# The opening of a two-layer attention encoder: zeros ahead of the first matmul, another queue for the norm weights, smaller first weight chunk, a fixed order

## The chip, the core and the metric

The kernel runs on one core of one Trainium2 chip. The core has five engines with a program each: TensorE (PE: matmuls, transposes), VectorE (DVE), ScalarE (ACT), GpSimd (POOL), and SyncE (SP), which issues most of the DMAs. An engine works through its own instructions in a fixed order and waits for others by semaphores. The metric is the device time of one execution in microseconds; lower is better.

## The reference

Two layers over 512 frames of width 1024. Each normalises its input by the root of the mean of squares, mixes the frames, adds the result, and then does the same with a wide squared-ReLU MLP. Layer 0 mixes by sparse attention: an indexer scores all keys for each query, the best 128 are kept, and 16 heads attend to those. Layer 1 is latent attention. A last norm follows. What the change touches is the start of layer 0:

```python
def rms_norm(x, g):
    xf = x.astype(jnp.float32)
    y = xf * lax.rsqrt(jnp.mean(xf * xf, axis=-1, keepdims=True) + EPS)
    return (y * g.astype(jnp.float32)).astype(x.dtype)

def dsa_mixer(h, w_in, w_out, cos_a, sin_a, cos_i, sin_i):
    proj = h @ w_in                                   # 512 x 1024 @ 1024 x 2120
    q, k, v, qi, ki, wi = jnp.split(proj, cuts, axis=-1)
    ...
    logits = jnp.einsum('bthd,bsd->bths', qib, ki, preferred_element_type=f32)
    score = jnp.einsum('bths,bth->bts', jax.nn.relu(logits), wib)
    _, sel = lax.top_k(score, top_k)
```

## The kernel before

The 512 frames lie in four tiles of 128 rows, worked in the order 1, 2, 3, 0. All weights and activations are split in a high and a low part of a shorter float type, and each product is three matmuls (`mm3`): high by high (L227), high by the weight's low part (L228), low by the weight's high part (L229). In the names of the profile, `w_hi` and `w_lo` are the parts of a weight chunk, `hT_hi` and `hT_lo` those of the activations with the features on the partitions.

`Weights` brings the weights in, chunk after chunk, in a list that `rows` fills. `fetch` starts the load of the next chunk into one of three raw buffers. `convert` makes the parts: ScalarE casts the high part (L143), and GpSimd ("ap") or VectorE ("av") subtracts it to get the low part (L150); there are five buffers for parts. `take` hands out the next chunk and converts others ahead of need, `held` fewer than the buffers would allow. The first three chunks hold the rows 0 to 2, 3 to 5 and 6 to 7 (of eight rows of 128) of 292 columns of `a_w_in`, the next three the same rows of 292 more.

The opening, in the code's order: loads of tile 1, of the norm weights (`g_row`, one row of 1024) and of the other tiles and chunks on SyncE's queue (L301 to L309); `g_ps` (L316): two matmuls with a row of ones spread the norm weights over 128 partitions; the constants `ident`, `smask`, `inv`. Then, for each tile, `gains` (L477, VectorE) multiplies by the norm weights into `h`; `turn` transposes `h` on TensorE by eight 128 x 128 transposes into `tps` (L454), ScalarE copies `hT_hi` from there (L458) and VectorE subtracts `hT_lo` (L459); `factor` lets ScalarE sum the squares (L483, `junk`), VectorE take the mean (L484, `lead`), and GpSimd the power -1/2 (L485). `idx_rows` projects tiles 1, 2 and 3 on the first 292 columns into the banks `ip`; `out_of` (L715) moves a finished `ip` to `inat`, scaled by the factor. `rope_tables` makes the rotary tables from the positions (L337 to L374: `posf`, `pos`, `ang`, `turns`, `sincos`). After that `idx_tile` projects the second 292 columns (64 of them for tile 0), then `proj_tiles` the remaining columns (`pp`); index scores (`lp`) come between, and the selection and the heads follow.

A scheduler in the framework orders each engine's instructions by data, priority and estimated times; the code's order is only where it starts from. The rest of the program is two MLPs and the second mixer, which the change doesn't touch.

## Time and profile before

| what | us |
|---|---|
| median of 3 runs | 1151.42 (1150.63 to 1152.6) |
| the profiled execution | 1150.95 |
| its span, from the first to the last instruction seen | 1149.2 |
| TensorE busy | 1117.5 |
| VectorE busy | 754.8 |
| GpSimd busy | 670.0 |
| ScalarE busy | 619.7 |

A row of a timeline names the start, the duration, the engine, the line, the operation and what it writes and reads; at its end stand the engine's idle time before it and what ended it. Matmuls are pipelined, so the distance of two starts (the pitch) tells more than the duration of one. The granted clock (PEclk) is a share of 2.4 GHz.

### The profile page before, as it was taken

What the parts mean: (1) busy time and instruction counts of PE and PEld (TensorE: products, weight loads), DVE (VectorE), ACT (ScalarE), POOL (GpSimd) and SP (SyncE); (2) the same over time, 40 slices, a digit from 0 to 9 for tenths busy, and PEclk for the clock granted to TensorE, in tenths of its full rate; (3) what the DMA queues carried; (4) which work ended last, traced back from release to release, by engine and by line L of the source; (5) the groups of instructions that cost most, each with busy time, mean ns of one, the idle gap of its engine ahead of it and who ended that gap; (6) DMA issues with size and microseconds to landing.
All of it is one profiled execution on the core that took longest, in us unless ns stands there. A gap on an engine that the chain in (4) does not pass through costs nothing.

```text
span 1149.2 us, 16018 instructions
## 1 busy us (share of the span) xinstructions
PE 1117.5 (97%) x5725; PEld 949.2 (83%) x5725; DVE 754.8 (66%) x1399; ACT 619.7 (54%) x1143; POOL 670.0 (58%) x508
## 2 busy tenths in 40 slices
PE   8999899989999999999999999899999999999997
PEld 7788788869888888888889898787988888888886
DVE  6699798673566466466566788676556466556664
ACT  6574896534544554454445776563564454464452
POOL 5498533543657857856702643554557756865772
PEclk9999999989999999999999999999999999999999
DMA  6413100242224314413322200111424313412402
GB/s 200 123 55 110 38 1 1 76 150 87 75 72 147 106 58 130 133 58 103 86 62 79 76 23 34 56 56 56 167 63 138 128 49 117 147 61 87 147 10 83
DMA packets 65465, 99.04 MB, mean 86 GB/s; under 512 B 3173, under 2 KB 41833, under 8 KB 65386
## 3 DMA queue, kind: packets, MB, share of 16 engines
q1 hardware_dynamic: 65386, 98.03, 26.9%
q8 instruction: 45, 0.74, 0.3%
q14 instruction: 34, 0.28, 0.1%
HBM read 95.92 MB, written 2.10 MB: 85 GB/s over the span
## 4 chain that ended last, share of the span: by engine, by line
PE 90%; DVE 3%; ACT 3%; issue 2%; POOL 1%; DMA 1%; SPq 0%; DVEq 0%; POOLq 0%; ACTq 0%
PE dn L1226 23%; PE up L227 10%; PE up L229 10%; PE up L228 10%; PE s_ps L560 3%; PE o_ps L622 3%; PE pt_ps L579 2%; PE wo_ps L227 2%; PE wo_ps L228 2%; PE wo_ps L229 2%; PE pp L227 2%; PE pp L229 2%; PE pp L228 2%; PE tps L454 1%; PE dn L228 1%
## 5 line engine op out<-in xcount | busy, mean ns | idle before, releaser
L148 POOL TENSOR_TENSOR w_lo<-quad,w_hi 128x512 fp32r<-128x512 f32 x196 | 274.7, 1433 | 163.1 <-ACT w_hi L143 155.7
L150 POOL TENSOR_TENSOR w_lo<-w_raw,w_hi 128x1024 fp32r<-128x1024 f32 (+4 forms) x117 | 264.4, 2278 | 86.7 <-ACT w_hi L143 71.6
L1229 DVE TENSOR_TENSOR x<-dn,x 128x512 f32<-128x512 f32 x196 | 134.9, 690 | 139.5 <-PE dn L1226 139.4
L228 PE MATMUL up<-hT_lo,w_hi 128*128 128x512 f32 (+1 forms) x576 | 210.8, 367 | 0.0
L227 PE MATMUL up<-hT_hi,w_hi 128*128 128x512 f32 (+1 forms) x576 | 210.3, 368 | 0.0
L229 PE MATMUL up<-hT_hi,w_lo 128*128 128x512 f32 (+1 forms) x576 | 208.8, 367 | 0.0
L143 ACT CAST w_hi<-w_raw 128x1024 fp32r<-128x1024 f32 (+6 forms) x112 | 111.7, 1006 | 141.1 <-PE dn L1226 62.2
L143 ACT CAST w_hi<-quad 128x1024 fp32r<-128x1024 f32 x98 | 101.2, 1050 | 100.0 <-DVE quad L86 71.7
L1226 PE MATMUL dn<-w_hi,lh 128*128 128x512 f32 x392 | 152.5, 389 | 0.0
L1226 PE MATMUL dn<-w_lo,lh 128*128 128x512 f32 x392 | 152.5, 389 | 0.0
L1226 PE MATMUL dn<-w_hi,ll 128*128 128x512 f32 x392 | 152.5, 389 | 0.0
L1191 DVE TENSOR_TENSOR ll<-u,lh 128x512 fp32r<-128x512 f32 x106 | 99.2, 966 | 40.7 <-ACT lh L1190 40.7
L229 PEld LDWEIGHTS up<-hT_hi,w_lo 128*128 128x128 f32 x576 | 109.1, 190 | 17.6
L227 PEld LDWEIGHTS up<-hT_hi,w_hi 128*128 128x128 f32 x576 | 109.0, 190 | 17.6 <-ACT hT_hi L458 0.2
L228 PEld LDWEIGHTS up<-hT_lo,w_hi 128*128 128x128 f32 x576 | 109.1, 190 | 17.4
L86 DVE TENSOR_TENSOR quad<-quad 128x1024 f32<-128x1024 f32 x56 | 68.4, 1221 | 65.3 <-POOL w_lo L148 65.3
L1190 ACT CAST lh<-u 128x512 fp32r<-128x512 f32 x106 | 62.9, 620 | 75.0 <-DVE u L1203 66.6
L1226 PEld LDWEIGHTS dn<-w_hi,ll 128*128 128x128 f32 x392 | 73.6, 188 | 15.3
L1226 PEld LDWEIGHTS dn<-w_hi,lh 128*128 128x128 f32 x392 | 73.6, 188 | 15.3
L1226 PEld LDWEIGHTS dn<-w_lo,lh 128*128 128x128 f32 x392 | 73.6, 188 | 15.3
L573 ACT ACTIVATE p<-p,m 128x128 f32<-128x128 f32 (+3 forms) x128 | 72.0, 564 | 16.3 <-DVE m L568 15.5
L592 ACT CAST pt_hi<-pt_ps 128x128 fp32r<-128x128 f32 (+3 forms) x128 | 53.0, 423 | 27.8 <-PE pt_ps L579 25.3
(237 smaller groups left out, 2249.8 us busy)
## 6 DMA issues: line engine op xcount, KB each, us to landing
w_raw<-in_mlp_w_up_dram SPq DMA_DIRECT2D x64, 512.0 KB, 3.7
quad<-in_mlp_w_down_dram SPq DMA_DIRECT2D x56, 512.0 KB, 3.6
w_raw<-in_a_w_in_dram SPq DMA_DIRECT2D x12, 512.0 KB, 3.6
w_raw<-in_a_w_out_dram SPq DMA_DIRECT2D x8, 512.0 KB, 3.2
w_raw<-in_mlp_w_down_dram SPq DMA_DIRECT2D x8, 512.0 KB, 4.5
w_raw<-in_b_w_out_dram SPq DMA_DIRECT2D x8, 512.0 KB, 3.7
x<-in_x_dram SPq DMA_DIRECT2D x4, 512.0 KB, 7.5
w_raw<-in_b_w_kv_up_dram SPq DMA_DIRECT2D x4, 512.0 KB, 3.9
```

Of the source, the lines that this page charges most:

```text
L86: self.nc.vector.tensor_sub(q[o], q[l], q[r])
L143: nc.scalar.copy(h, v)
L148: nc.gpsimd.tensor_sub(l[:, cs], v[:, cs], h[:, cs].bitcast(F32))
L150: (nc.gpsimd if engs[1] == "p" else nc.vector).tensor_sub(l, v, h.bitcast(F32))
L227: nc.tensor.matmul(ps, lh, rh, start=first, stop=False)
L228: nc.tensor.matmul(ps, lh, rl, start=False, stop=False)
L229: nc.tensor.matmul(ps, ll, rh, start=False, stop=last)
L573: nc.scalar.activation(U["p"][:, :N], U["p"][:, :N], AF.Exp, bias=U["m"], scale=-1.0, accum_out=pair["sums"][:, c:c + 1])
L1190: nc.scalar.copy(lh, v)
L1191: nc.vector.tensor_sub(ll, v, lh.bitcast(F32))
L1226: nc.tensor.matmul(pp[t], l[:, k, ts], r[:, k, :], start=first and k == 0 and m == 0, stop=k == 1 and m == 2, skip_group_check=True)
L1229: last = nc.vector.tensor_add(x[:, cs], pp[t], x[:, cs])
```

## The change

Seven things are changed, all ahead of the second set of index columns:

1. `smask` is zeroed by VectorE as the first thing, and seven matmuls of 128 x 128 zeros (`rest`) stand on TensorE ahead of `g_ps`.
2. `g_row` and the positions are loaded on ScalarE's queue; `g_row` is that engine's first instruction, ahead of its table load.
3. Tile 1 is loaded in two halves.
4. The first 292 columns come in four chunks, of 1, 2, 3 and 2 rows, in place of three of 3, 3 and 2. The third is subtracted by VectorE ("av"), the others by GpSimd. Two chunks are fetched right behind tile 1.
5. The opening's order on TensorE, ScalarE and VectorE is that of the code. `take(1, 4)` converts the chunk that is taken and none beyond it; `ahead` is new and converts a given number beyond.
6. The sums of squares (`squares`) are apart from mean and power (`factor`) and stand later.
7. The rotary tables are issued behind the last `hT_lo`.

```diff
+    def ahead(self, n):
+        while len(self.done) < min(self.taken + n, len(self.items)):
+            self.convert()
...
+    smask = const.tile([P, 512], F32, name="smask")
+    nc.vector.memset(smask[:, 0:P], 0.0)
+    nc.vector.memset(smask[:, P:512], 0.0)
+    with tc.high_priority(400):
+        rest = bank("rest", 7)
+        for _ in range(7):
+            nc.tensor.matmul(rest[:, 0:P], smask[:, 0:P], smask[:, 0:P], start=True, stop=True)
...
-    W.rows(a_w_in[0][0:3 * P], 1536, 1828, 3, "av")
-    W.rows(a_w_in[0][3 * P:6 * P], 1536, 1828, 3, "ap")
-    W.rows(a_w_in[0][6 * P:8 * P], 1536, 1828, 2, "ap")
+    W.rows(a_w_in[0][0:P], 1536, 1828, 1)
+    W.rows(a_w_in[0][P:3 * P], 1536, 1828, 2)
+    W.rows(a_w_in[0][3 * P:6 * P], 1536, 1828, 3, "av")
+    W.rows(a_w_in[0][6 * P:8 * P], 1536, 1828, 2)
...
+    g_row = ht.tile([1, D], F32, name="g_row", tag="h", bufs=2)
+    nc.scalar.dma_start(g_row, attn_norm[0:1])
     for t in (1, 2, 3, 0):
-        nc.sync.dma_start(xt[t], x[0, t * P:(t + 1) * P, :])
+        for c in range(2 if t == 1 else 1):
+            cs = slice(c * 512, (c + 1) * 512) if t == 1 else slice(0, D)
+            nc.sync.dma_start(xt[t][:, cs], x[0, t * P:(t + 1) * P, cs])
+        W.fetch()
         if t == 1:
-            g_row = ht.tile([1, D], F32, name="g_row", tag="h", bufs=2)
-            nc.sync.dma_start(g_row, attn_norm[0:1])
-        W.fetch()
+            W.fetch()
...
-    nc.sync.dma_start(posi, positions.rearrange("o (t p) -> (o t) p", p=P))
+    nc.scalar.dma_start(posi, positions.rearrange("o (t p) -> (o t) p", p=P))
...
-    nc.gpsimd.memset(smask, 0.0)
...
+                with tc.manual_schedule(engines={mybir.EngineType.PE, mybir.EngineType.Activation,
+                                                 mybir.EngineType.DVE}):
+                    nm.gains(1)
+                    w0, w1 = W.take(1, 4)[0], W.take(1, 4)[0]
+                    nm.turn(1)
+                    idx_rows(1, 0, w0)
+                    idx_rows(1, 1, w1)
+                    nm.gains(2)
+                    nm.turn(2)
+                    w2 = W.take(1, 4)[0]
+                    idx_rows(2, 0, w0)
+                    idx_rows(2, 1, w1)
+                    nm.squares(pr, 1)
+                    idx_rows(1, 3, w2)
+                    nm.gains(3)
+                    nm.turn(3)
+                    nm.squares(pr, 2)
+                    idx_rows(2, 3, w2)
+                    idx_rows(3, 0, w0)
+                    idx_rows(3, 1, w1)
+                    idx_rows(3, 3, w2)
+                    nm.gains(0)
+                    turned = nm.turn(0)
+                    w3 = W.take(1, 4)[0]
+                    nm.squares(pr, 3)
+                    W.ahead(1)
+                    for t in range(1, NT):
+                        idx_rows(t, 6, w3)
+                        nm.factor(t)
+                        out_of(inat[t][:, :292], ips[t][:, :292], t)
+                        W.ahead(t + 1)
+                        if t == 1:
+                            nm.squares(pr, 0)
+                    nm.factor(0)
+                with tc.issue_after(turned.ins):
+                    rope_tables()
```

What moves on the engines. ScalarE, from the first cast of a weight chunk on, before (a line number, the operation, what it writes and reads, its shape; `x_85` is tile 1, `x_86` tile 2, `x_87` tile 3, `x_84` tile 0):

```order
L143 CAST w_hi<-w_raw 128x876
L483 ACTIVATE junk,lead<-x_86 128x1024
L143 CAST w_hi<-w_raw 128x876
L458 CAST hT_hi<-tps 128x4x128
L483 ACTIVATE junk,lead<-x_87 128x1024
L458 CAST hT_hi<-tps 128x4x128
L143 CAST w_hi<-w_raw 128x584
L458 CAST hT_hi<-tps 128x4x128
L483 ACTIVATE junk,lead<-x_84 128x1024
L143 CAST w_hi<-w_raw 128x876
L458 CAST hT_hi<-tps 128x4x128
L143 CAST w_hi<-w_raw 128x876
```

ScalarE at the same place now (`x_96` is tile 1, `x_97` tile 2, `x_98` tile 3; 292, 584, 876 and 584 columns are the four chunks of the first set, the next 876 the first of the second set):

```order
L148 CAST w_hi<-w_raw 128x292
L148 CAST w_hi<-w_raw 128x584
L475 CAST hT_hi<-tps 128x4x128 x4
L148 CAST w_hi<-w_raw 128x876
L499 ACTIVATE junk,lead<-x_96 128x1024
L475 CAST hT_hi<-tps 128x4x128 x2
L499 ACTIVATE junk,lead<-x_97 128x1024
L475 CAST hT_hi<-tps 128x4x128 x2
L148 CAST w_hi<-w_raw 128x584
L499 ACTIVATE junk,lead<-x_98 128x1024
L148 CAST w_hi<-w_raw 128x876
L735 ACTIVATE inat_146<-ip,lead 128x292
```

The casts of the third and fourth chunk stand behind copies of `hT_hi` (four and eight of them), where before all three chunks of the first set were cast by the third copy.

GpSimd, from the first weight chunk or power on, before:

```order
L485 TENSOR_TENSOR lead<-lead,neghalf 128x1
L150 TENSOR_TENSOR w_lo<-w_raw,w_hi 128x876
L485 TENSOR_TENSOR lead<-lead,neghalf 128x1
L150 TENSOR_TENSOR w_lo<-w_raw,w_hi 128x584
L485 TENSOR_TENSOR lead<-lead,neghalf 128x1 x2
L150 TENSOR_TENSOR w_lo<-w_raw,w_hi 128x876 x2
L150 TENSOR_TENSOR w_lo<-w_raw,w_hi 128x584
```

GpSimd there now:

```order
L155 TENSOR_TENSOR w_lo<-w_raw,w_hi 128x292
L155 TENSOR_TENSOR w_lo<-w_raw,w_hi 128x584 x2
L505 TENSOR_TENSOR lead<-lead,neghalf 128x1 x3
L155 TENSOR_TENSOR w_lo<-w_raw,w_hi 128x876 x2
L505 TENSOR_TENSOR lead<-lead,neghalf 128x1
L155 TENSOR_TENSOR w_lo<-w_raw,w_hi 128x584
```

Three powers stand between the last chunk of the first set and the first of the second, and the power of tile 0 ahead of the last chunk of the second set.

TensorE around the last transposes of tile 0, before:

```order
L227 MATMUL ip<-w_hi,hT_hi 128x292
L454 MATMUL tps<-ident,h 128x128 x4
L229 MATMUL ip<-w_hi,hT_lo 128x292
L227 MATMUL ip<-w_hi,hT_hi 128x292
L228 MATMUL ip<-w_lo,hT_hi 128x292
L229 MATMUL ip<-w_hi,hT_lo 128x292
```

TensorE there now (`pos_ps` is the transpose of the positions for the rotary tables):

```order
L234 MATMUL ip<-w_hi,hT_lo 128x292
L471 MATMUL tps<-ident,h 128x128 x8
L232 MATMUL ip<-w_hi,hT_hi 128x292
L359 MATMUL pos_ps<-ident,posf 128x4
L233 MATMUL ip<-w_lo,hT_hi 128x292
L234 MATMUL ip<-w_hi,hT_lo 128x292
```

The eight transposes stand together, and the first matmuls behind them are those of the fourth chunk; before, four and four stood among matmuls of chunks made earlier. On VectorE the operations of the rotary tables (posf to sincos) stand behind the last `hT_lo`, and the mean of tile 0 behind them. The scheduler also gives TensorE another order of the heads in the first mixer (the same matmuls and transposes, about 200 rows of the order). Elsewhere no engine's order differs.

## Rows read from the trace of the kernel before

**Rows 1.** The page: busy time by engine; the chain that ended last, by engine.
```profile
PE 1117.5 (97%) x5725; PEld 949.2 (83%) x5725; DVE 754.8 (66%) x1399; ACT 619.7 (54%) x1143; POOL 670.0 (58%) x508
...
PE 90%; DVE 3%; ACT 3%; issue 2%; POOL 1%; DMA 1%; SPq 0%; DVEq 0%; POOLq 0%; ACTq 0%
```

**Rows 2.** Timeline of TensorE, opening: start us, duration us, operation [idle before, releaser].
```profile
4.26 3.75 PE L316 MATMUL g_ps<-g_row,one_row 1*128 1x512 f32 x4 [4.26 <-DMA g_row<-in_attn_norm_dram]
7.94 2.26 PE L454 MATMUL tps<-ident,h 128*128 128x128 f32 x8
10.72 0.61 PE L227 MATMUL ip<-w_hi,hT_hi 128*128 128x292 f32 x1 [0.52 <-ACT hT_hi L458]
...
13.09 0.45 PE L229 MATMUL ip<-w_hi,hT_lo 128*128 128x292 f32 x1
13.33 0.45 PE L227 MATMUL ip<-w_hi,hT_hi 128*128 128x292 f32 x1
...
14.64 0.29 PE L227 MATMUL ip<-w_hi,hT_hi 128*128 128x292 f32 x1
14.78 0.30 PE L228 MATMUL ip<-w_lo,hT_hi 128*128 128x292 f32 x1
...
37.39 0.48 PE L227 MATMUL pp<-w_hi,hT_hi 128*128 128x512 f32 x1
```

**Rows 3.** Stretches: us, busy (count) of PE, PEld, DVE, ACT, POOL, PEclk, DMA, GB/s.
```profile
4.20:14.30 10.10, 9.49 (x26) 5.94 (x27) 7.37 (x14) 8.22 (x15) 4.58 (x5) 1.00 0.91 316
118.00:123.70 5.70, 2.16 (x11) 1.16 (x9) 1.91 (x6) 5.62 (x13) 4.96 (x8) 1.00 0.13 42
123.70:127.10 3.40, 3.23 (x15) 2.98 (x15) 2.60 (x10) 3.03 (x11) 0.00 (x0) 0.50 0.31 124
247.90:249.97 2.07, 0.03 (x1) 0.00 (x0) 1.95 (x2) 1.95 (x4) 2.07 (x3) 1.00 1.08 400
249.97:256.80 6.83, 5.12 (x23) 4.93 (x24) 5.67 (x7) 2.83 (x5) 3.91 (x3) 0.50 0.99 314
```

**Rows 4.** Timeline of GpSimd, opening: low parts of weights, powers.
```profile
12.85 1.44 POOL L150 TENSOR_TENSOR w_lo<-w_raw,w_hi 128x584 fp32r<-128x584 f32 x1
...
15.10 0.55 POOL L485 TENSOR_TENSOR lead<-lead,neghalf 128x1 f32<-128x1 f32 x1 [0.31 <-DVE lead L484]
15.61 4.11 POOL L150 TENSOR_TENSOR w_lo<-w_raw,w_hi 128x876 fp32r<-128x876 f32 x2
```

**Rows 5.** Timeline of ScalarE, opening: squares, casts, copies.
```profile
8.15 1.06 ACT L483 ACTIVATE junk<-x 128x1024 bf16<-128x1024 f32 x1 [0.82 <-DMA x<-in_x_dram]
...
9.26 0.92 ACT L143 CAST w_hi<-w_raw 128x876 fp32r<-128x876 f32 x1
10.09 0.58 ACT L458 CAST hT_hi<-tps 128x512 fp32r<-128x512 f32 x1
...
12.09 0.68 ACT L143 CAST w_hi<-w_raw 128x584 fp32r<-128x584 f32 x1
```

**Rows 6.** Stretches behind the opening, columns as in rows 3.
```profile
60.00:118.00 58.00, 58.00 (x270) 47.72 (x269) 55.77 (x150) 33.72 (x64) 50.14 (x65) 1.00 0.29 89
118.00:124.00 6.00, 2.29 (x12) 1.23 (x10) 2.21 (x8) 5.92 (x14) 4.96 (x8) 0.97 0.17 57
124.00:160.00 36.00, 34.27 (x221) 29.75 (x222) 32.58 (x100) 32.33 (x97) 11.87 (x11) 0.96 0.03 10
```

**Rows 7.** Timeline of VectorE, opening.
```profile
7.36 1.07 DVE L150 TENSOR_TENSOR w_lo<-w_raw,w_hi 128x876 fp32r<-128x876 f32 x1 [0.33 <-ACT w_hi L143]
...
12.56 0.68 DVE L459 TENSOR_TENSOR hT_lo<-tps,hT_hi 128x512 fp32r<-128x512 f32 x1
...
17.68 2.50 DVE L347 TENSOR_SCALAR ang<-inv,pos 128x24 f32<-128x24 f32 x4
...
20.70 0.19 DVE L354 TENSOR_SCALAR turns<-ang 128x96 f32<-128x96 f32 x1
...
22.64 0.74 DVE L360 SCALAR_TENSOR_TENSOR ang<-turns,ang 128x192 f32<-128x192 f32 x2
```

More of the change, by code (lines that the diff above doesn't have):

```diff
@@ L319, in trunk @@
     make_identity(nc, ident)
-    smask = const.tile([P, 512], F32, name="smask")
-    nc.gpsimd.memset(smask, 0.0)
     nc.gpsimd.memset(smask[0:CHUNK, 512 - CHUNK:512], NEG)
@@ L458, in to_feature_major @@
             nc.scalar.copy(h, pv)
-            nc.vector.tensor_sub(l, pv, h.bitcast(F32))
+            last = nc.vector.tensor_sub(l, pv, h.bitcast(F32))
+        return last
     class Norm:
@@ L477, in gains, with squares, factor @@
                 nc.vector.tensor_mul(h[:, cs], xt[t][:, cs], self.g[c])
-        def factor(self, pool, t):
+        def squares(self, pool, t):
             junk = pool.tile([P, D], mybir.dt.bfloat16, name="junk", tag="junk", bufs=1)
+            nc.scalar.activation(junk, xt[t], AF.Square, accum_out=lead[:, 2 * t:2 * t + 1])
+        def factor(self, t):
             ss, y = lead[:, 2 * t:2 * t + 1], lead[:, 2 * t + 1:2 * t + 2]
             self.y[t] = y
-            nc.scalar.activation(junk, xt[t], AF.Square, accum_out=ss)
             nc.vector.tensor_scalar(y, ss, 1.0 / D, EPS, op0=OP.mult, op1=OP.add)
@@ L492, in turn @@
             with tc.high_priority(60):
-                to_feature_major(self.h.pop(t), KD, self.hi, self.lo, t, self.banks)
+                return to_feature_major(self.h.pop(t), KD, self.hi, self.lo, t, self.banks)
         def follow(self, t, c):
@@ L728, in idx_tile @@
                     out_of(inat[t][:, a0 - QI0:a1 - QI0], ps[:, :a1 - a0], t)
-                nm.gains(1)
-                nm.turn(1)
-                w0 = W.take(1, 2)[0]
-                idx_rows(1, 0, w0)
-                nm.gains(2)
-                nm.turn(2)
-                nm.factor(pr, 1)
-                idx_rows(2, 0, w0)
-                w1 = W.take(1, 2)[0]
-                idx_rows(1, 3, w1)
-                nm.gains(3)
-                nm.turn(3)
-                nm.factor(pr, 2)
@@ L743, in mixer_a @@
-                idx_rows(3, 0, w0)
-                idx_rows(2, 3, w1)
-                idx_rows(3, 3, w1)
-                nm.gains(0)
-                nm.turn(0)
-                rope_tables()
-                nm.factor(pr, 3)
-                w2 = W.take(1, 2)[0]
-                for t in range(1, NT):
-                    idx_rows(t, 6, w2)
-                    out_of(inat[t][:, :292], ips[t][:, :292], t)
-                nm.factor(pr, 0)
+                with tc.manual_schedule(engines={mybir.EngineType.PE, mybir.EngineType.Activation,
[32 more added lines that the diff above has]
+                    nm.factor(0)
```

## The prediction

> **What bounds the kernel now.** The page of the profile comes first: TensorE is busy for 97% of the span and is 90% of the chain that ended last [rows 1]. So the time is TensorE's work plus its waits, and an edit in the opening counts by how much it moves the first matmul of the projections, `pp`. That one starts at 37.39 us [rows 2]. Next, the rows of TensorE: it stands idle for 4.26 us until the norm weights have landed, spends 3.75 us on their broadcast, 2.26 us on eight transposes, waits 0.52 us, and starts the index projection at 10.72 us [rows 2]. From there to 37.39 us nothing holds it up: 144 matmuls of 292 columns, 24 of 64 and 24 transposes run back to back. Their pitch is 0.24 us at first (13.09 to 13.33) and 0.14 us later (14.64 to 14.78) [rows 2]. The granted clock reads 1.00 for all of that stretch [rows 3], so here the pitch, not the clock column, tells the level: TensorE runs at 1.2 GHz until about 14.4 us and at 2.4 GHz after it. What the opening has to give is thus the 4.26 us, the low level until 14.4 us, and little more; what it has to lose is the 23 us behind that, in which TensorE never waits.
>
> It doesn't wait there since the weights are ready early. GpSimd makes the low parts: `w_lo` of the third chunk at 12.85 us, the next two from 15.61 to 19.72 us [rows 4]; ScalarE casts that third chunk at 12.09 us [rows 5]. With each chunk made ahead of its user, no wait on a `w_lo` stands in TensorE's rows.
>
> Does a delay at `pp` come through? From 60 to 118 us TensorE is busy for 58.00 of 58 us and VectorE for 55.77; from 118 to 160 us TensorE idles 3.71 + 1.73 us [rows 6]. There is nothing before 118 us to absorb a delay, so I carry it whole to the end.
>
> **The change, part by part.** *Zeros and norm weights.* Seven matmuls of zeros go ahead of the broadcast. The broadcast is two matmuls of 512 columns in 3.75 us, 1.88 us each, in the same plain fp32 as the zeros, so 128 columns are about 0.47 us, and the seven last 7 x 0.47 = 3.3 us, from about 1 to 4.3 us. The norm weights, issued 0.4 us sooner on ScalarE's queue, land at some 3.8 us instead of 4.2. The broadcast then starts behind the zeros at 4.3 us, as before: gain 0. ScalarE gives a DMA issue ahead of its table load and has nothing else to do before tile 1 lands, cost 0. The first index matmul comes earlier, since ScalarE no longer casts and squares between the transposes and `hT_hi`: 0.52 us of wait and part of the copies go, first matmul at about 10.0 us, **-0.75 us**.
>
> *Clock.* If zeros count as work, TensorE is at work from 1 us instead of 4.3, and the rise that came 10 us after the start of work would come near 11 us; if they don't, near 14.4. Before, 3.7 us of index matmuls ran low (10.72 to 14.4) and lost half of that, 1.85; after, it is 0.5 to 2.2. I take **-0.5 us**, bounds -1.35 to +0.35; a rise at once behind the zeros is a rival.
>
> *Fixed order and chunks.* The work is the same: 168 matmuls, 32 transposes. But each chunk is now converted where the order takes it, with no look-ahead, and every conversion is ScalarE's cast, then GpSimd's (or VectorE's) `w_lo`, queued behind that place. Five waits of TensorE on `w_lo` follow, none of which exists now:
> - third chunk (VectorE): behind the last `hT_hi` of tile 2 (0.58) come cast 0.92 and `w_lo` 1.07 [rows 5, 7]; TensorE has nine matmuls meanwhile, 1.2 us fast or 2.2 us slow. Wait 0.4 to 1.4, taken **1.0**.
> - fourth chunk (GpSimd): its cast stands behind the last `hT_hi` of tile 0 on ScalarE. After the last transpose: 0.58 + 0.68 + 1.44 = 2.7 us [rows 4, 5]; TensorE has one matmul and a tiny transpose. Wait **2.6**.
> - fifth: GpSimd must do three powers (0.55 each) and 2.05 behind that, 3.7 us [rows 4]; TensorE has 17 + 1 matmuls x 0.135 = 2.4. Wait **1.3**.
> - sixth: 2.05 against nine matmuls, 1.2. Wait **0.85**.
> - seventh: ahead of it on GpSimd stands the power of tile 0, which needs VectorE's mean of squares, and that stands behind the whole chain of rotary angles on VectorE. The angle operations are small, but next to a `w_lo` they don't run: four `ang` that should take 0.13 us each took 2.50 us, from 17.68 to 20.18, while GpSimd worked until 19.72; with GpSimd idle, the next of the chain, at 20.70, took 0.19 us on four times the columns [rows 4, 7]. So the chain stands until the sixth `w_lo` is done, and then takes about 2.7 us (ten operations, 0.19 to 0.37 us each [rows 7]), mean 0.15, power 0.55, `w_lo` 1.44: 4.8 us against nine matmuls of 1.2. Wait **3.6**; without that blocking the chain is through by then and the wait is 0.55 + 1.44 - 1.2 = 0.8.
>
> The Trainium skill says in "SBUF — State Buffer", section "SBUF: two separate sides", that VectorE and GpSimd share a pair of ports as an exclusive lock for a whole instruction; the `ang` row agrees (2.50 us for four). By that rule the seventh wait would be the longer one, which is the one taken from the rows.
>
> Sum of the waits: 1.0 + 2.6 + 1.3 + 0.85 + 3.6 = **+9.35 us**.
>
> *Clock in the waits.* At 118 us TensorE worked 2.16 of 5.7 us and then the granted clock was 0.50 for 3.4 us; at 248 us it worked 0.03 of 2.07 us and the clock was 0.50 for 6.83 us [rows 3]. Between tile 0's transposes and the seventh chunk it works some 5 of 14 us. A fall in the last wait costs half of 3.4 to 6.8 us less what of it passes in the wait: 0 to 3.4 us, taken **+1.0**.
>
> *The rest.* Halves of tile 1, the position load on another queue, and the rotary tables behind the transposes: the first users (`inat`, after the index projection) come later than the tables, 0. Zeroing of the mask goes to VectorE, which has no input yet: 0. The scheduler puts the attention heads of the first mixer in another order on TensorE (about 131 to 158 us); same work, so 0, bounds -2 to +2 (idle there is 1.73 us [rows 6]).
>
> Sum: -0.75 - 0.5 + 9.35 + 1.0 = **+9.1 us**, and `pp` starts at about 46.5 us. On the profiled execution, 1150.95 us, that gives 1160.0 us; the median of the runs is 0.47 us above that execution, which is within what the terms leave open.
>
> **Rivals.**
> - *B: the angle chain isn't held.* For: an `hT_lo` took its usual 0.68 us at 12.56, beside the `w_lo` of 12.85 [rows 4, 7], so not all of VectorE is blocked. Against: the rows above. The seventh wait is 0.8, and with no wait above 2.6 us the clock stays: 1160.0 - 2.8 - 1.0 = 1156.2 us.
> - *C: the zeros bring the high level at once.* For: they are 3.3 us of work without a gap, and after 123.7 us it took 3.4 us of work (3.23 busy) for the clock to return [rows 3]. Against: before, 9.49 of 10.10 us of work stood ahead of the rise [rows 3]. Broadcast, 16 transposes and 9 matmuls would be 1.9 + 2.2 + 1.0 = 5 us shorter, but tile 2 lands only at 8.1 us [rows 5] and the waits on conversions grow by about half of the 5 us: 1160.0 - 2.0 to 2.7, about 1157.6 us. The Trainium skill ("TensorE: Matmul & The Clock Gate", part 1, "What's actually happening") holds the throttled state for the default that activity lifts; it would make C's condition true, and no row here shows zeros as that activity.
> - *D: the clock falls already in the fourth chunk's wait and stays low through the 64-column tail and the first `pp`.* +3.4 in place of +1.0: 1162.4 us.
> - *E, the other side: the new order of the heads takes the idle time of 118 to 160 us.* Place: TensorE, softmax waits of the first heads. Price: at most 3.71 + 1.73 us idle and 1.7 us (half of 3.4) of low clock, 7.1 us. Against it: the first of these waits is on the first head's own softmax, with no other work at hand. It decides only where the opening costs under 7.1 us, so together with B: 1156.2 - 7.1 = 1149.1 us; with the forecast it is 1152.9.
> - *F: the delay doesn't come through,* since the selection on VectorE (55.77 of 58 us [rows 6]) sets the end at 118 us and starts when it did. Against: it needs the index scores, which stand on TensorE behind the first `pp`. Within 2 us of 1151.
>
> **How the numbers follow.** Forecast 0.48 (own range 1158 to 1162), B 0.15, C 0.12, D 0.10, E 0.10, F 0.05. The likeliest gives 1160.0. The range reaches down to 1155.0 (B less 1.2) and up to 1164.0 (D and 1.6 of the heads' order); outside are E, F and an end of D. About 2 us (0.2%) is what can be told from no change. Faster by more: 0.08 of E and 0.02 of F, 0.10. Within: 0.02 of E and 0.03 of F, 0.05. Slower: 0.85.
>
> **What would show it.** In the changed kernel's trace: TensorE idle ahead of the matmul that reads `w_lo`, once with VectorE and four times with GpSimd as releaser, of 1.0, 2.6, 1.3, 0.85 and 3.6 us; first broadcast still at 4.3 us; first `pp` near 46.5 us. The pitch of the index matmuls tells the clock: 0.24 us up to 11 or 14 us speaks for the forecast, 0.13 us from the start for C. VectorE's angle operations that end with a `w_lo` of GpSimd speak against B. TensorE idle between 118 and 160 us (shifted by 9 us) far under 5.4 us speaks for E. I am wrong altogether if `pp` starts before 39 us, or if it starts near 46 us and the span grows by less than 5 us.

## The result

| | before | changed |
|---|---|---|
| median of 4 runs | 1151.9 us (1150.63 to 1152.6) | 1162.03 us (1159.48 to 1164.13) |
| ratio of the runs | 1 | 1.0081, 95% interval 1.0069 to 1.0094 |
| the profiled execution | 1150.95 us | 1162.86 us |
| its span | 1149.2 us | 1160.9 us |

The changed kernel is slower by 0.8%: 9.3 us by the ratio, 10.1 us by the two medians. The prediction was 1160.0 us with a range of 1155 to 1164. The two profiled executions lie further apart than the ratio says, 11.9 us; executions of the changed kernel spread over 4.7 us.

TensorE in the opening of the changed kernel, rows of its timeline (start us, duration us, operation, idle before and releaser); they answer [rows 2]:

```profile
1.04 3.35 PE L244 MATMUL rest<-smask 128*128 128x128 f32 x14 [1.04 <-DVE smask L237]
4.33 3.78 PE L335 MATMUL g_ps<-g_row,one_row 1*128 1x512 f32 x4
8.04 1.97 PE L471 MATMUL tps<-ident,h 128*128 128x128 f32 x8
9.83 0.61 PE L232 MATMUL ip<-w_hi,hT_hi 128*128 128x292 f32 x1
...
11.94 0.45 PE L233 MATMUL ip<-w_lo,hT_hi 128*128 128x292 f32 x1
12.18 0.35 PE L234 MATMUL ip<-w_hi,hT_lo 128*128 128x292 f32 x1
12.37 1.03 PE L471 MATMUL tps<-ident,h 128*128 128x128 f32 x8
...
16.06 0.40 PE L233 MATMUL ip<-w_lo,hT_hi 128*128 128x292 f32 x1 [0.35 <-DVE w_lo L155]
...
21.73 1.03 PE L471 MATMUL tps<-ident,h 128*128 128x128 f32 x8
24.07 0.40 PE L232 MATMUL ip<-w_hi,hT_hi 128*128 128x292 f32 x1 [1.30 <-ACT w_hi L148]
25.65 0.22 PE L359 MATMUL pos_ps<-ident,posf 4*128 4x4 f32 x1 [1.18 <-DVE posf L357]
25.80 0.51 PE L233 MATMUL ip<-w_lo,hT_hi 128*128 128x292 f32 x1
...
31.22 0.40 PE L233 MATMUL ip<-w_lo,hT_hi 128*128 128x292 f32 x1
...
35.43 0.40 PE L233 MATMUL ip<-w_lo,hT_hi 128*128 128x292 f32 x1 [2.73 <-POOL w_lo L155]
...
46.74 0.48 PE L232 MATMUL pp<-w_hi,hT_hi 128*128 128x512 f32 x1
```

The broadcast starts where it did, the first index matmul 0.9 us sooner, and from there on come the waits: 0.35 us on the third chunk, 1.30 + 1.18 us behind the transposes of tile 0, 2.73 us ahead of the seventh chunk. The row at 31.22 us is that of the sixth chunk's low part. The first `pp` starts at 46.74 us, 9.35 us later than before.

What two of those waits bring along shows in the stretches (us; busy of PE, PEld, DVE, ACT, POOL with counts; PEclk; DMA; GB/s), to be held against [rows 3]:

```profile
25.80:29.40 3.60, 3.60 (x16) 3.60 (x16) 3.38 (x10) 2.09 (x4) 3.60 (x5) 0.53 0.30 83
29.40:36.00 6.60, 3.86 (x27) 3.39 (x26) 6.03 (x14) 3.66 (x8) 4.33 (x4) 1.00 0.56 159
36.00:39.50 3.50, 3.50 (x17) 3.50 (x16) 3.50 (x2) 0.90 (x2) 3.50 (x2) 0.53 0.71 172
```

TensorE works without a gap in the first and the third, at a granted clock of 0.53: the clock has fallen behind the waits, twice, for some 3.4 us each time.

VectorE and GpSimd at the same time (their timelines), to be held against [rows 4, 7]:

```profile
24.31 1.29 DVE L357 CAST posf<-posi 4x128 f32<-4x128 int32 x1
...
27.00 0.20 DVE L375 COPY ang<-ang 128x96 f32<-128x96 f32 x1
27.12 2.08 DVE L372 TENSOR_SCALAR turns<-turns 128x96 f32<-128x96 f32 x1
29.23 2.05 DVE L373 TENSOR_SCALAR turns<-turns 128x192 f32<-128x192 f32 x1
31.32 0.26 DVE L374 TENSOR_SCALAR turns<-turns 128x192 f32<-128x192 f32 x1
...
48.80 2.43 DVE L410 TENSOR_TENSOR rope_u<-inat,ropeC_a 128x16 f32<-128x16 f32 x1
51.26 2.28 DVE L411 TENSOR_TENSOR inat<-rope_u,rope_v 128x16 f32<-128x16 f32 x1
```

```profile
24.10 1.43 POOL L155 TENSOR_TENSOR w_lo<-w_raw,w_hi 128x584 fp32r<-128x584 f32 x1 [14.64 <-ACT w_hi L148]
...
27.08 4.09 POOL L155 TENSOR_TENSOR w_lo<-w_raw,w_hi 128x876 fp32r<-128x876 f32 x2
33.44 0.59 POOL L505 TENSOR_TENSOR lead<-lead,neghalf 128x1 f32<-128x1 f32 x1 [2.27 <-DVE lead L504]
...
46.43 7.08 POOL L155 TENSOR_TENSOR w_lo<-w_raw,w_hi 128x1024 fp32r<-128x1024 f32 x3 [6.35 <-ACT w_hi L148]
```

Two operations of the rotary angles last just as long as the two `w_lo` of 27.08 to 31.17 us beside them; GpSimd's idle time of 2.27 us ahead of the power is the rest of the angle chain. It happens again at 48.80 and 51.26 us, to the rotary step of tile 0. Before, the second of these operations was held as well, but the first got through (VectorE of the kernel before):

```profile
39.44 0.16 DVE L393 TENSOR_TENSOR rope_u<-inat,ropeC_a 128x16 f32<-128x16 f32 x1
39.63 2.26 DVE L394 TENSOR_TENSOR inat<-rope_u,rope_v 128x16 f32<-128x16 f32 x1
```

One more operation held, 2.43 in place of 0.16 us, and now the transposes of `kip` wait for that step (TensorE of the changed kernel):

```profile
53.69 0.60 PE L846 MATMUL kip<-ident,inat 128*64 128x128 f32 x4 [1.58 <-DVE inat L411]
55.55 0.49 PE L885 MATMUL lp<-ki,qis 128*128 128x512 f32 x1
...
132.48 0.33 PE L599 MATMUL pt_ps<-ident,p 128*128 128x128 f32 x1 [2.33 <-ACT p L593]
...
263.24 1.94 PE L471 MATMUL tps<-ident,h 128*128 128x128 f32 x8 [3.75 <-DVE h L443]
```

The same places before: the first index scores `lp`, the same softmax wait, the transposes ahead of the first MLP.

```profile
44.46 0.49 PE L853 MATMUL lp<-ki,qis 128*128 128x512 f32 x1
...
121.33 0.33 PE L579 MATMUL pt_ps<-ident,p 128*128 128x128 f32 x1 [2.32 <-ACT p L573]
...
251.68 1.94 PE L454 MATMUL tps<-ident,h 128*128 128x128 f32 x8 [3.74 <-DVE h L426]
```

So the changed kernel is behind by 9.35 us at `pp`, 11.09 at `lp`, 11.15 at the first heads, 11.56 at the MLP, 11.7 at the end of the span. After `lp` only 0.6 us more are lost.

### The profile page after: what moved, and what is told of

It reads as the page before. It is cut to its first block, busy times and chain, and to the rows that moved or that the text cites. A ratio compares the mean times of both kernels' runs of the same rounds, so it can differ in the third digit from the quotient of the medians.

```text
span 1160.9 us, 16059 instructions
## 1 busy us (share of the span) xinstructions
PE 1124.9 (97%) x5739; PEld 953.7 (82%) x5739; DVE 772.1 (67%) x1401; ACT 618.3 (53%) x1144; POOL 671.2 (58%) x508
## 4 chain that ended last, share of the span: by engine, by line
PE 84%; DVE 5%; issue 4%; ACT 3%; POOL 3%; POOLq 0%; DVEq 0%; ACTq 0%
PE dn L1258 22%; PE up L232 9%; PE up L233 9%; PE up L234 9%; PE o_ps L642 3%; PE s_ps L580 3%; PE pt_ps L599 2%; PE wo_ps L232 2%; PE wo_ps L233 2%; PE wo_ps L234 2%; PE pp L234 2%; PE pp L232 2%; PE pp L233 2%; POOL w_lo L153 2%; PE tps L471 1%
## 5 line engine op out<-in xcount | busy, mean ns | idle before, releaser
L155 POOL TENSOR_TENSOR w_lo<-w_raw,w_hi 128x1024 fp32r<-128x1024 f32 (+5 forms) x118 | 265.3, 2269 | 104.6 <-ACT w_hi L148 101.8
L148 ACT CAST w_hi<-w_raw 128x1024 fp32r<-128x1024 f32 (+7 forms) x113 | 111.9, 998 | 152.2 <-PE dn L1258 63.0
```

The costliest lines, as they stand in the source:

```text
L148: nc.scalar.copy(h, v)
L155: (nc.gpsimd if engs[1] == "p" else nc.vector).tensor_sub(l, v, h.bitcast(F32))
```

## The experiments

Theory: the loss is the place of the conversions in the engines' queues, and the angle chain that GpSimd's low parts hold up. Rivals: the fixed order by itself (transposes in blocks of eight), the clock with the zeros, the new order of the heads. All landmarks are starts in us in the profiled execution.

| kernel | broadcast | first `pp` | first `lp` | MLP transposes | ratio to before (95%) |
|---|---|---|---|---|---|
| before | 4.26 | 37.39 | 44.46 | 251.68 | 1 |
| changed | 4.33 | 46.74 | 55.55 | 263.24 | 1.0081 (1.0069 to 1.0094) |
| e1, fourth chunk early | 4.33 | 45.41 | 52.50 | 259.74 | 1.0079 (1.0062 to 1.0096) |
| e2, mean ahead of angles | 4.33 | 43.45 | 55.52 | 263.32 | 1.0094 (1.0078 to 1.0111) |
| e3, both | 4.33 | 43.42 | 52.47 | 260.11 | 1.0083 (1.0067 to 1.0100) |
| e4, no zeros | 2.33 | 45.87 | 52.95 | 261.04 | 1.0070 (1.0045 to 1.0094) |
| e9, no fixed order | 4.33 | 37.32 | 44.39 | 251.69 | 1.0033 (1.0021 to 1.0045) |
| e12, second set by VectorE | 4.33 | 43.94 | 51.01 | 258.72 | 1.0092 (1.0070 to 1.0114) |
| e5, before + zeros | 4.38 | 36.63 | 43.72 | 251.04 | 1.0012 (1.0000 to 1.0023) |
| e6, before + norm weights' queue | 2.22 | 35.84 | 42.91 | 250.19 | 0.9996 (0.9988 to 1.0005) |
| e10, e6 + halves + two zeros | 2.49 | 36.88 | 45.70 | 253.07 | 0.9996 (0.9988 to 1.0005) |
| e11, fixed order, parts early | 2.33 | 35.92 | 48.10 | 254.01 | 1.0041 (1.0026 to 1.0055) |
| e13, the same, casts first | 2.33 | 36.89 | 47.07 | 255.18 | 1.0024 (1.0013 to 1.0036) |
| e14, e6 + small chunk | 2.24 | 37.27 | 46.07 | 253.63 | 0.9998 (0.9989 to 1.0007) |

**The fixed order (e9).** The changed kernel with the three engines given back to the scheduler:

```diff
-                with tc.manual_schedule(engines={mybir.EngineType.PE, mybir.EngineType.Activation,
-                                                 mybir.EngineType.DVE}):
+                if True:
```

> The changed kernel without the fixed order: the code is the same, but the scheduler orders TensorE, ScalarE and VectorE. It puts the cast of the fourth chunk behind the third copy of hT_hi in place of the eighth, and the mean of tile 0 ahead of the angles. If the fixed order makes the loss, TensorE's waits on low parts go but for GpSimd's rate, pp comes at 37 to 39 us and the first index scores at 45 to 47 (44.46 before, 55.55 changed). If the chunks and missing look-ahead make it by themselves, pp stays above 43. The time follows the index scores, plus up to 2.4 us, since the scheduler gives the second mixer the order that cost that much in the run with the fourth chunk early.

The landmarks are those of the kernel before, to 0.1 us:

```profile
37.32 0.48 PE L232 MATMUL pp<-w_hi,hT_hi 128*128 128x512 f32 x1
...
44.39 0.49 PE L884 MATMUL lp<-ki,qis 128*128 128x512 f32 x1
```

So the whole loss of 11 us at `lp` comes with the fixed order; zeros, queue and chunks together neither gain nor lose there. The time is still 0.33% (3.8 us) above before. 2.1 us of that are as expected: the scheduler gives the second mixer another order in this kernel, as in e1, e3, e11 and e12, and there the output projection waits (view of TensorE's waits of e1, about 750 to 862 us: total, times, longest; before has 0.3 us in that row, e9 the same 2.4 as e1):

```profile
PE wo_ps L232 <- DVE x L551: 2.4, 3, 0.8
```

The other 1.7 us of e9 stay open.

**Is it the order as such, or where the conversions stand in it? (e1, e11, e13)** e1 moves one conversion:

```diff
-                    w2 = W.take(1, 4)[0]
+                    w2 = W.take(1, 3)[0]
```

> The changed kernel with one edit: the fourth chunk of the first 292 columns is converted right behind the third, ahead of tiles 3 and 0, in place of behind tile 0's copies. If the loss is made by conversions that stand late in the engines' queues, TensorE's idle of 1.30 + 1.18 us behind tile 0's transposes goes (it has 17 matmuls at once), GpSimd reaches the fifth chunk about 1.5 us sooner, and the wait moves there: first pp near 44 us (46.74 in the changed kernel), time 2 to 4 us less than the changed kernel. If instead the granted clock makes the loss, the wait on the fifth chunk is as long as the one that went, the clock falls as before, and pp stays within 1 us of 46.7. If the new order of the heads makes it, pp moves but the span doesn't.

`pp` moved by 1.3 us, between what the theory and the clock rival expected: the 2.5 us of waits behind tile 0's transposes are gone, and a wait of 2.34 us stands at the fifth chunk instead. `lp` came 3.05 us sooner: 1.33 us of that is the gain at `pp`, the rest comes since one operation more of tile 0's rotary step got through between the low parts, as in the kernel before. The time didn't follow: 2.1 of the 3.5 us that e1 is ahead at the MLP are given back in `wo_ps`.

e11 takes the zeros out and places every cast a tile earlier, squares and powers as soon as a tile has landed:

```diff
+                    nm.squares(pr, 1)
+                    nm.factor(1)
                     nm.gains(1)
...
                     idx_rows(1, 0, w0)
                     nm.gains(2)
+                    w2 = W.take(1, 4)[0]
                     idx_rows(1, 1, w1)
                     nm.turn(2)
-                    w2 = W.take(1, 4)[0]
+                    nm.squares(pr, 2)
...
+                    w3 = W.take(1, 4)[0]
+                    nm.factor(2)
                     nm.gains(3)
...
+                    W.ahead(1)
+                    nm.factor(3)
                     nm.gains(0)
...
-                    w3 = W.take(1, 4)[0]
+                    nm.squares(pr, 0)
+                    nm.factor(0)
+                    W.ahead(2)
```

> The changed kernel without zeros and with another fixed order: each chunk is cast ahead of the copies of the next tile, one tile sooner than its user, the squares of a tile as soon as it has landed, mean and power of tile 0 ahead of the angles. If a fixed order costs by itself (transposes in blocks of eight), pp stays above 38 us. If only the place of the conversions costs, no wait on a low part over 0.5 us is left, and with the broadcast from 2.3 us the first pp comes at 34 to 36 us (37.39 before) and the index scores at 41 to 43 (44.46). Time: 1 to 2 us less than before by that, plus 2.4 us for the scheduler's other order of the second mixer: within 1 us of before.

No wait on a low part was left, and `pp` came at 35.92 us, as early as in e6 below (35.84), which has the early broadcast without a fixed order. So a fixed order with blocks of eight transposes doesn't cost by itself up to `pp`; the place of the conversions, squares and powers does (the three were moved together here, so no run tells them apart). The index scores were missed by 5 us, though, and the time, expected within 1 us of before, is 0.41% longer: the rotary steps on VectorE now met the low parts of the `pp` chunks, and TensorE waits for them (its timeline in e11):

```profile
43.84 0.33 PE L835 MATMUL qip<-ident,inat 128*128 128x128 f32 x1 [3.32 <-DVE inat L406]
```

e13 is e11 with two lines exchanged:

```diff
+                    W.ahead(2)
                     nm.squares(pr, 0)
                     nm.factor(0)
-                    W.ahead(2)
```

> As the run with the early parts in a fixed order, but the two casts of the second set stand ahead of the squares of tile 0. The opening is the same within 0.5 us; the scheduler happens to keep the second mixer's order of before for this one. If that order is what cost 2.2 to 2.4 us in the runs that had it, this one is that much faster: 1 to 3 us less than before (index scores at 41 to 43 us in place of 44.46). If not, both runs have the same time.

The waits in `wo_ps` are back to 0.3 us, and e13 is 1.9 us faster than e11 by the means of their runs, though its MLP starts 1.2 us later. That fits 2 to 3 us for the second mixer's order, but weakly: the intervals of the two ratios, 1.0024 and 1.0041, overlap. It isn't faster than before, since the rotary steps hold `lp` here too (2.90 us).

**The angle chain (e2, e3, e12).** e2 issues the rotary tables behind the mean of tile 0:

```diff
...
-                    nm.factor(0)
-                with tc.issue_after(turned.ins):
+                    meant = nm.factor(0)
+                with tc.issue_after(meant.ins):
```

> The changed kernel with one edit: VectorE's mean of tile 0 stands ahead of the rotary tables, in place of behind them. Theory of the blocked angle chain: GpSimd does the power of tile 0 right behind the sixth low part (31.2 us), the seventh is ready at 33.2 instead of 35.4 us, TensorE's wait of 2.73 us shrinks to about 0.6 and the clock doesn't fall a second time: first pp near 43 us, 3 to 4 us less than 46.74. Rival, the chain is not what holds GpSimd there: the wait stays above 2 us and pp within 0.5 us of 46.7. The angle operations themselves stay slow beside low parts (about 2 us each) by both.

`pp` at 43.45 us: the seventh chunk's wait fell from 2.73 to 0.21 us, and the clock theory's `pp` of 46.7 is out. And yet `lp` stands at 55.52 us, where it stood. The tables are now late, the rotary steps of the other tiles run into the low parts of the `pp` chunks, and TensorE waits 3.33 us ahead of `qip`:

```profile
43.45 0.48 PE L232 MATMUL pp<-w_hi,hT_hi 128*128 128x512 f32 x1
47.63 0.38 PE L838 MATMUL qip<-ident,inat 128*128 128x128 f32 x2
51.34 0.47 PE L838 MATMUL qip<-ident,inat 128*128 128x128 f32 x1 [3.33 <-DVE inat L411]
```

This is a wait exchanged for another, and the time says so: no gain.

> The two edits together: fourth chunk early, mean of tile 0 ahead of the angles. By the theory of the queues the waits that remain are GpSimd's rate alone (2.05 us for a chunk that TensorE uses in 1.2): fifth about 2.5, sixth 0.85, seventh 0.8 us. First pp near 42 us, time 4 to 6 us less than the changed kernel and still 3 to 5 us more than the kernel before. By the clock theory it is no better than the better one of the two edits.

Both edits together are no better at `pp` than e2 alone (43.42), not 42 as expected: `pos_ps`, in TensorE's order ahead of the fifth chunk, now waits 2.39 us for the positions on VectorE, which stand behind the mean of tile 0. `lp` is that of e1. The time, expected 4 to 6 us below the changed kernel, is the same (1.0083 against 1.0081).

e12 takes the cause away in another manner; the low parts of the second set go to VectorE:

```diff
-    W.rows(a_w_in[0], 1828, 2120, KD)
+    W.rows(a_w_in[0], 1828, 2120, KD, "av")
```

> The changed kernel with the low parts of the second 292 columns subtracted by VectorE in place of GpSimd. Theory of the shared port: GpSimd has no long instruction while the angle chain runs, so each angle operation takes 0.2 to 0.4 us in place of 2.05 to 2.08; the powers of the factors aren't behind low parts; the wait of 2.73 us ahead of the seventh chunk falls to 1 to 2 us (its low part now stands behind the rotary tables on VectorE), pp comes near 45 us (46.74). If the angle operations are slow for another reason, they stay at 2 us and pp gets later, since VectorE now has three low parts more. The scheduler gives the second mixer the order that cost 2.4 us, so the time is no better than the changed kernel's by more than 1 us.

The two operations that took 2.08 and 2.05 us are back to 0.20 and 0.26 us, in the same place of the program (VectorE's timeline in e12):

```profile
28.08 0.20 DVE L372 TENSOR_SCALAR turns<-turns 128x96 f32<-128x96 f32 x1
28.32 0.26 DVE L373 TENSOR_SCALAR turns<-turns 128x192 f32<-128x192 f32 x1
```

That they were held by GpSimd's low parts is shown by this; `pp` came 2.8 us sooner, more than expected, although VectorE has 2.9 us of low parts more. The time shows nothing of the 4.5 us by which the MLP starts sooner (258.72 against 263.24). From there to the end it took 904.0 us against 897.7. One stretch of 50 us, 500 us behind the MLP's start, has some of that (changed kernel, then e12):

```profile
763.24:813.24 50.00, 49.67 (x275) 41.99 (x274) 35.91 (x85) 24.53 (x62) 26.43 (x19) 1.00 0.21 64
```

```profile
758.72:808.72 50.00, 47.61 (x259) 40.28 (x258) 32.06 (x79) 23.41 (x61) 25.09 (x17) 0.96 0.21 64
```

2.1 us are `wo_ps` waits, and a granted clock of 0.96 over 50 us is 4 us at half speed, some 2 us lost. The other 2 us stay open; over the whole span the granted clock of this execution is 0.988, of the changed kernel's 0.992.

**Zeros and queue (e4, e5, e6, e10, e14).** e4 is the changed kernel without the zeros:

```diff
-    with tc.high_priority(400):
-        rest = bank("rest", 7)
-        for _ in range(7):
-            nc.tensor.matmul(rest[:, 0:P], smask[:, 0:P], smask[:, 0:P], start=True, stop=True)
```

> The changed kernel without the seven matmuls of zeros. If they count as work for the clock, the fast pitch (0.135 us) comes near 14 us instead of 12.2, and what runs before that (the transposes of tile 2, 8 x 0.13 us lost, a few matmuls) takes up to 1.5 us longer; against that the broadcast starts when the norm weights land, near 4.0 instead of 4.33 us. The later waits take up part of either, so pp moves by -0.3 to +1 us. If the zeros do nothing, the fast pitch comes at the same 12.2 us and pp is 0.3 us sooner.

```profile
2.33 3.75 PE L330 MATMUL g_ps<-g_row,one_row 1*128 1x512 f32 x4 [2.33 <-DMA g_row<-in_attn_norm_dram]
```

The norm weights land at 2.3 us. The zeros keep TensorE until 4.4 us and so take back the 2.0 us that the other queue gave; without them `pp` is 0.87 us sooner and `lp` 2.6. The expectation, -0.3 to +1 us, was made with the landing at 4.0 us and missed for that reason. The fast pitch came within the eight transposes of 11.05 us (1.49 us, where eight take 1.97 at the low level and 1.03 at the high one). With the zeros it came from 12.2 us (changed kernel) to some 14 us (e3). So no gain of the zeros for the clock shows here.

e5 puts the same lines, and the two lines that zero `smask` on VectorE, into the kernel before:

```diff
...
+        for _ in range(7):
+            nc.tensor.matmul(rest[:, 0:P], smask[:, 0:P], smask[:, 0:P], start=True, stop=True)
```

> The kernel before plus the seven matmuls of zeros (and VectorE's zeroing of the mask) alone. The norm weights come on SyncE's queue as before and land at 4.2 us, the zeros end at 4.4 us, so the broadcast starts within 0.2 us of where it did. If zeros count as work, the pitch of 0.135 us comes near 12.2 us in place of 14.4 and the first pp about 1 us sooner (36.4 against 37.39): time 0.5 to 1.2 us less. If they don't count, pp stays within 0.3 us.

`pp` is 0.76 us sooner, within the expectation, but by another way (TensorE's timeline in e5):

```profile
4.38 1.95 PE L326 MATMUL g_ps<-g_row,one_row 1*128 1x512 f32 x4
6.51 0.63 PE L462 MATMUL tps<-ident,h 128*128 128x128 f32 x4 [0.18 <-POOL lead L493]
8.31 1.11 PE L462 MATMUL tps<-ident,h 128*128 128x128 f32 x4 [1.17 <-DVE h L485]
```

Here the broadcast takes 1.95 us in place of 3.75 and four transposes 0.63: 2.4 GHz right behind the zeros. Then TensorE waits for the second half of tile 1's `h`, which stands behind a low part on VectorE, and the next four transposes take 1.11 us, at 1.2 GHz again. Of the seven profiled kernels with seven zeros, two show the high level right behind them (e5; e9 with a broadcast of 2.36 us), five don't (broadcast 3.78 us). In both it was lost again behind the next wait, 1.17 us for `h` in e5 and 1.60 us for `hT_hi` in e9. In the time nothing is gained: 1.0012, with an interval that ends at 1.0000.

e6 moves the load of the norm weights alone:

```diff
+    g_row = ht.tile([1, D], F32, name="g_row", tag="h", bufs=2)
+    nc.scalar.dma_start(g_row, attn_norm[0:1])
     for t in (1, 2, 3, 0):
         nc.sync.dma_start(xt[t], x[0, t * P:(t + 1) * P, :])
-        if t == 1:
-            g_row = ht.tile([1, D], F32, name="g_row", tag="h", bufs=2)
-            nc.sync.dma_start(g_row, attn_norm[0:1])
```

> The kernel before with the load of the norm weights on ScalarE's queue alone; the order of TensorE, VectorE and GpSimd is that of before. They land at 2.3 us, as they did without the zeros, and the broadcast starts 1.9 us sooner. If the opening is a chain from the broadcast on, the first index matmul comes near 9 us (10.72) and pp near 36 (37.39): time 1 to 1.9 us less. If the loads of the tiles and of the first chunk are late enough to hold it (tile 1 at 4.5, first chunk at 6.4 us), pp moves by less than 0.5 us.

Broadcast at 2.22, `pp` at 35.84, `lp` at 42.91, the MLP at 250.19 us: 1.5 us sooner everywhere, the size that the first theory had. But the chain from the broadcast on isn't what passes it on. ScalarE has the squares of tile 2 and a cast ahead of the first `hT_hi`, and the squares wait for the load of tile 2: until 8.15 us before [rows 5], until 6.86 us in e6 (ScalarE's timeline):

```profile
6.86 1.06 ACT L482 ACTIVATE junk<-x 128x1024 bf16<-128x1024 f32 x1 [0.53 <-DMA x<-in_x_dram]
```

The first index matmul is sooner by the same 1.3 us (9.44 against 10.72); e14 below has the same early broadcast, tile 2 as late as before, and no gain there. The load of tile 2 was issued only 0.3 us sooner (1.65 against 1.98 us), so why it landed so much sooner stays open. In the runs the gain is -0.04%, interval -0.12 to +0.05%; a gain of 1.5 us (0.13%) lies just outside of that, so what the trace shows at the MLP isn't confirmed by the time. It is the part of the change that does no harm.

e10 adds to e6 the halves of tile 1 and two zeros:

```diff
...
+        for _ in range(2):
+            nc.tensor.matmul(rest[:, 0:P], smask[:, 0:P], smask[:, 0:P], start=True, stop=True)
...
+        for c in range(2 if t == 1 else 1):
+            cs = slice(c * 512, (c + 1) * 512) if t == 1 else slice(0, D)
+            nc.sync.dma_start(xt[t][:, cs], x[0, t * P:(t + 1) * P, cs])
```

> The kernel before with the norm weights on ScalarE's queue, tile 1 in two halves, and two matmuls of zeros in place of seven, which end at 2.0 us, ahead of the norm weights. If zeros count, the fast pitch comes near 11 us and the broadcast at 2.3 us: first pp near 35 us, time 2 to 3 us less than before, and less than either edit alone. If the idle time between zeros and broadcast makes them worthless, it equals the run with the norm weights alone.

Two zeros that end at 2.3 us gave no early clock. The first weight chunk landed at 7.0 us (before 6.4 us), and the second half of tile 1's `h` stands behind its low part on VectorE, so the transposes of tile 1 waited 2.43 us; `pp` at 36.88, `lp` later than before. No gain over e6.

e14 adds the small chunk to e6, with the scheduler's order and look-ahead:

```diff
+    W.rows(a_w_in[0][0:P], 1536, 1828, 1)
+    W.rows(a_w_in[0][P:3 * P], 1536, 1828, 2)
+    W.rows(a_w_in[0][3 * P:6 * P], 1536, 1828, 3)
+    W.rows(a_w_in[0][6 * P:8 * P], 1536, 1828, 2, "av")
...
+                wa = W.take(1, 2)[0]
+                idx_rows(1, 1, wa)
...
```

> The kernel before with two parts of the change that looked like its gain, and the scheduler's order and look-ahead kept: norm weights on ScalarE's queue, and the first 292 columns in chunks of 1, 2, 3 and 2 rows (the last subtracted by VectorE, the others by GpSimd). Theory: the broadcast starts at 2.3 us and the second half of tile 1's product is no longer behind VectorE's first low part, so the first index matmul comes near 8.7 us (9.44 with the norm weights alone, 10.72 before), first pp at 34.5 to 36 us (37.39), index scores at 41.5 to 43 (44.46), and the time is 1.5 to 3 us less than before. Rival: the loads of tiles 2 and 3 (8.1 us and later) hold it, and it is no better than the norm weights alone: pp at 35.8 us, and the time can't be told from before.

A miss, and near the rival: as in e6, ScalarE has the squares of tile 2 and a cast of 876 columns ahead of the first `hT_hi`, but here tile 2, whose load now stands behind two chunks, lands at 8.17 us, as late as before. With the broadcast at 2.24 us the first index matmul is where it was before (ScalarE, then TensorE):

```profile
8.17 1.06 ACT L485 ACTIVATE junk<-x 128x1024 bf16<-128x1024 f32 x1 [1.28 <-DMA x<-in_x_dram]
...
10.71 0.61 PE L227 MATMUL ip<-w_hi,hT_hi 128*128 128x292 f32 x1 [2.38 <-ACT hT_hi L460]
```

No kernel here beats the one before by more than the measurement can tell. And the landmarks tell the time only to some 2 us: e10 and e14 reach the MLP 1.4 and 2.0 us later than the kernel before, and their time isn't longer (0.9996 and 0.9998).

## Why the prediction was right, and which terms were off

*The place and the sign.* The waits are where the conversions were put, and the loss goes through to the end (rival F is out): 9.35 us at `pp` (forecast 9.1), 46.74 us (forecast 46.5). e9 and e11 together show the cause: without the fixed order, or with conversions, squares and powers earlier in it, the loss at `pp` is gone. At `lp` e11 keeps 3.6 us of it, by the rotary steps.

*Head start, -0.75.* Measured -0.89 (9.83 against 10.72). Right in size, but one of its terms was wrong: "land at some 3.8 us" should have been 2.3 (e4). The zeros, put down at 0, cost 2.0 us of broadcast and 0.87 at `pp`. The estimate took only the earlier issue (0.4 us) off the landing and not that on SyncE's queue the row stood behind tile 1's 512 KB.

*Clock at the start, -0.5.* The fast pitch came at 12.2 us, 11 us after the first zero; forecast "near 11" or 14.4. Nine matmuls at about 0.26 us lost 1.15 us in place of 1.85: -0.7. The size fits; that the zeros are the reason isn't shown, since e4 had the fast pitch as early without them.

*Five waits, +9.35.* Measured 0.35, 2.48, 0, 0 and 2.73: 5.6 us, and 0.43 us of small waits for `hT`. The first lies below its bounds of 0.4 to 1.4. The second and the last are right in place, the last in its releaser too; the second shows as a wait for the cast and one for `posf`, which lasted 1.29 us beside the fourth low part (0.20 us in e1, with GpSimd idle) and so hides that part. The fifth and the sixth chunk's waits, 1.3 and 0.85, hardly showed: after 2.5 us of waiting the clock had fallen, TensorE took 0.24 us a matmul, and GpSimd kept up. The sixth low part, done at 31.17 us, still set its matmul at 31.22 us, 0.17 us later than the pitch would have it. So the same time was lost, under another name.

*Clock in the waits, +1.0.* It fell twice, not once. From 25.8 to 29.45 and from 36.1 to 39.6 us, some 14.5 matmuls each at 0.24 in place of 0.135 us: 1.5 + 1.5 = 3.0 us. So mechanism D, fall in the fourth chunk's wait, was right in its place, but the clock was back at 29.45 us and didn't stay low to the first `pp`; its price was mostly paid out of the waits behind it.

*Sum.* -0.9 - 0.7 + 6.0 + 3.0 = 7.4; the other 1.9 us are restarts. A wait costs TensorE more than its idle row: the matmul ahead of it runs out (0.30 in place of a pitch of 0.135), the first behind it takes 0.1 longer to the next. Seven such places at 0.27 are 1.9 us; this part is an estimate from the pitches, not tested by a run. That the sum came within 0.3 us of `pp` is luck in part: the waits were put 3.8 us too long, the clock in them 2.0 us too cheap, and the restarts at nothing.

*Rival B* (the angle chain isn't held) is out by e12. The Trainium skill's rule ("SBUF — State Buffer", section "SBUF: two separate sides": VectorE, in some of its operations, and GpSimd hold a shared pair of ports in turn, for a whole instruction) agrees with 2.05 to 2.08 us beside a low part and 0.20 to 0.26 us without one. The wait that hangs on it was 2.73 us, forecast 3.6: by the end of the sixth low part the chain was done up to the two held operations, so some 2.2 us of it were left, mean included, where the prediction had 2.85; and the nine matmuls took 1.5 us, not 1.2.

*Rival C* (zeros bring the high level) held in two of seven profiles, and was lost at the next wait. The Trainium skill says that activity releases the low state ("TensorE: Matmul & The Clock Gate", part 1, "What's actually happening"); e5 agrees, with a broadcast of 1.95 us, and the changed kernel's own profile doesn't show it, with 3.78 us behind the same zeros.

*Rival E* (the heads' new order pays): the same softmax waits, 2.33 us the longest, stand 11.15 us later; the MLP is 0.4 us later still. It doesn't pay.

*What failed:* "the first users (`inat`, after the index projection) come later than the tables, 0". The tables held up the rotary step of tile 1 (its `inat` was done at 36.94 us, the step began at 40.16), which no wait of TensorE shows. But one operation more of tile 0's rotary step met a low part, 2.43 in place of 0.16 us, and `kip` waited 1.58 us; at `lp` the loss is 11.09 us, 1.7 more than at `pp`. "I carry it whole" was right from `lp` on and not from `pp` on. The time came out near the forecast all the same: 9.3 us by the ratio of the runs, 10.1 by the medians, against 9.1. The profiled execution, 11.9 us behind, is one of the slower of the changed kernel and one of the faster of before, so its trace tells the places and not the size to better than 2 us.

## What to carry to other kernels

A fixed order fixes the queues of the helpers too: ahead of each matmul that needs a prepared operand, look at what the preparing engines have in front of it, and give them the lead that the scheduler's look-ahead gave. A small operation of VectorE between large ones of GpSimd can be priced by the large one. And carry a delay from the last instruction that everything behind it needs (here the first index scores), not from the first one that you can see move: three edits moved `pp` by 3 us and the time by none.

## What the runs showed of the hardware

- A load of 4 KB on ScalarE's queue landed 1.5 us after its issue (0.73 to 2.2 us); on SyncE's queue, behind a load of 512 KB, 3.1 us (1.17 to 4.26).
- Seven matmuls of zeros, 3.3 us without a gap, were followed by the high clock at once in two of seven profiles and some 8 to 10 us later in five.
- Between two long instructions of GpSimd none or one small one of VectorE got through in the rows shown, and the next stood for the whole of the following one: 2.05 to 2.43 us for operations that take 0.16 to 0.3 alone. An `hT_lo`, which reads `tps`, took its 0.68 us all the same (at 17.08 us of the kernel before, beside the low parts of 15.61 to 19.72 us).
- The profile's clock column read 1.00 in the opening (4.2 to 14.3 us of the kernel before) where the pitch of 0.24 us shows 1.2 GHz; later in the program, as at 25.8 us of the changed kernel, column and pitch agree.
